# Input loads, square sums and modulation columns at the start of layer 0 of a two-layer hybrid trunk

## The chip, the cores and the metric

The kernel runs on one NeuronCore of one Trainium2 chip. The metric is the device time of one execution in microseconds. The engines are named as in the profile: PE (TensorE) multiplies matrices, PEld is its weight load, DVE is VectorE, ACT is ScalarE, POOL is GpSimd, and SP only issues loads and stores.

## The reference, cut to what matters

Two layers run one after the other on x of 512 positions and 1024 features. Each layer normalises x, scales and shifts it with columns made from a conditioning vector c, multiplies by a wide matrix, runs three attention mixers, and adds the gated result to x:

```
mod = silu(c) @ w_ada + b_ada
shift, scale, gate = split(mod, 3)
u = rms_norm(x, norm_g) * (1 + scale) + shift
z = u @ w_in                      # all queries, keys, values and gates
y = three mixers on z
x = x + gate * (merge(y) @ w_out)
```

rms_norm divides by the root of the mean of the squares of a position's 1024 features. Everything is float32. The change touches the start: the loads of x, the squares, shift and scale of layer 0, and u.

## The kernel before

**Layout.** x is kept transposed: features on the 128 partitions, in eight blocks of 128 (k or j from 0 to 7), positions along the free dimension (512). A float32 product is made of three: u is split into uh (rounded) and ul (the rest), a weight into whi and wlo, and TensorE adds whi with uh, whi with ul and wlo with uh.

**Start.** `start` (lines 1419 to 1483) makes silu(c) and spreads it over a tile csr. Its inner function `norm` (line 1440) is called once for the first 256 positions and once for the second 256 (HALVES). It issues four loads of x (two blocks each, 256 KB, into the tiles vc and va), squares each piece on ScalarE into a tile t, adds the squares up, and lets TensorE sum them over the partitions by a multiplication with a matrix of -1. For the first half VectorE adds all pieces and TensorE does one multiplication; for the second half VectorE or GpSimd adds the two blocks of a piece, and TensorE does four. `rstd_of` (line 761) then makes the inverse root with Ln and Exp on ScalarE. `times_rstd` (765) multiplies x by it on VectorE. `make_u` (768) writes uh and a copy e, each as x * amul + mods, on ScalarE or VectorE, and ul = e - uh.

**Modulation of layer 0.** `ada_load(j)` (718) loads two pieces of 512 KB of w_ada for block j into tiles Y, of which there are five. `ada_first(j)` (723) forms two sums of 1024 products on VectorE, one for shift and one for scale, adds the bias columns into mods, and makes amul = (1 + scale) * norm_g.

**First phase.** `first_phase` (906) runs over the eight blocks. Per block it multiplies seven 128-column tiles of w_in (FIRST) with u: 21 multiplications into seven PSUM banks. In layer 0 blocks 0 and 1 are done in halves of 256 positions (`two0`), the others at the full 512. Before block k + 1 come its modulation, times_rstd and make_u. The weights of a block are two pieces (256 and 192 KB) that go through four wstage tiles and are split by a cast (whi) and a subtraction (wlo). After the first phase come the value projections (`v_phase`), then the mixers, the other projections and the output.

**What sets the order.** The program is first written into a `Recorder` (244) as a list of instructions. `add` (274) derives which instruction must wait for which from the elements of each tile that a view covers; `View.region` (191) gives a view's range of partitions and one range of elements, from the lowest to the highest. `forward` (379) then simulates the engines with a price per instruction (`price`, 307). Where an instruction names two engines, it goes to the one that would end it first. `latest` (500) gives due times, and after five rounds (`order`, 526) the best order is written out (`emit`, 539): each engine's queue runs in that fixed order. SP's queue is ordered in the same way. All emitted instructions carry the line 549, so the profile is read by tiles.

```
        whole = self.tile.at
        p0, f0 = divmod(self.at.__array_interface__["data"][0] - whole.__array_interface__["data"][0], whole.shape[1])
        free = list(zip(self.at.strides[1:], self.at.shape[1:]))
        lo = f0 + sum(min(0, s * (n - 1)) for s, n in free)
        hi = f0 + sum(max(0, s * (n - 1)) for s, n in free) + 1
        return p0, p0 + self.at.shape[0], lo, hi
```

A load of the second half of blocks 0 and 1 writes elements 256 to 511 and 768 to 1023 of its tile; region() calls that 256 to 1023. Elements 512 to 767 are the first half of block 1.

Of the kernel before, what the change touches and what calls it, by code (L numbers as in the profile page):

```python
# [25 lines left out]
F32 = mybir.dt.float32  # L26
F32R = mybir.dt.float32r
BF16 = mybir.dt.bfloat16
AF = mybir.ActivationFunctionType
OP = mybir.AluOpType  # L30

D = 1024
S = 512
P = 128
# [119 lines left out]
class View:  # L154
# [30 lines left out]
    def real(self):  # L185
# [2 lines left out]
            ap = ap.rearrange(arg, a=more[0]) if more else getattr(ap, name)(arg)  # L188
        return ap

    def region(self):

        whole = self.tile.at
# [5 lines that stand above are left out]
# [45 lines left out]
class Recorder:  # L244
# [29 lines left out]
    def add(self, ways):  # L274
        x = Instr()
        x.i = len(self.list)
        op, args, kw = next(iter(ways.values()))
        if op == "pairs":
            named = [(("out", "in", "in")[n], v) for q in args for n, v in enumerate(q)]
        else:  # L280
            named = [("out" if "out" not in kw and n == 0 else n, v) for n, v in enumerate(args)] + list(kw.items())
        x.writes = [v for n, v in named if isinstance(v, View) and n in ("out", "accum_out")]
        x.reads = [v for n, v in named if isinstance(v, View) and n not in ("out", "accum_out")]
        x.preds, x.succs = {}, []
        for views, w in ((x.reads, False), (x.writes, True)):
            for v in views:
                t, r = v.tile, v.region()
                if op == "matmul" and w and kw["start"]:
                    r = (r[0], r[1], 0, S)
                keep = []  # L290
                for (j, r2, w2) in t.seen:
                    over = r[0] < r2[1] and r2[0] < r[1] and r[2] < r2[3] and r2[2] < r[3]
                    if over and j is not x and (w or w2):
                        x.preds[j.i] = j
                    if not (w and over and r[0] <= r2[0] and r2[1] <= r[1] and r[2] <= r2[2] and r2[3] <= r[3] and j is not x):
                        keep.append((j, r2, w2))
                t.seen = keep + [(x, r, w)]
        x.tiles = list({id(v.tile): v.tile for v in x.reads + x.writes if not v.tile.pool.fixed}.values())
        for j in x.preds.values():
            j.succs.append(x)  # L300
        x.alts = {}
        for e, (op, args, kw) in ways.items():
            x.alts[e] = self.price(x, e, op, args, kw)
        x.prio = x.i
        self.list.append(x)
# [266 lines left out]
def trunk(ctx, tc, xT, vecs, w_ss, w_gt, w_first, w_t, w_v, w_br, w_o, rope, consts, out):  # L572
# [6 lines left out]
    rec = Recorder(tc, nc, ps, sb)  # L579
    PE, ACT, DVE, POOL, SP = (rec.engine(e) for e in ("PE", "ACT", "DVE", "POOL", "SP"))  # L580

    def fixed(name, shape, dt=F32):
        return rec.fixed(const.tile(shape, dt, name=name))
# [7 lines left out]
    def ybank():  # L591
        return rec.tile("ps_s", [P, S])
# [4 lines left out]
    def mm(o, lhsT, rhs, start, stop=True):  # L597
        PE.matmul(o, lhsT, rhs, start=start, stop=stop, skip_group_check=True)
# [5 lines left out]
    f = lambda ap: ap.bitcast(F32)  # L604
# [14 lines left out]
    def both(out, a, b, op_):  # L619
        how = ("tensor_tensor", (), dict(out=out, in0=a, in1=b, op=op_))  # L620
        rec.add({"DVE": how} if in_psum(a, b) else {"POOL": how, "DVE": how})
# [12 lines left out]
    csb, o = small[:, 0:8], 8  # L634
    g_sb = [small[:, o + 8 * l:o + 8 * l + 8] for l in range(L)]
    fg_sb, o = small[:, o + 8 * L:o + 8 * L + 8], o + 8 * L + 8
    b_ada, o = [small[:, o + 24 * l:o + 24 * l + 24] for l in range(L)], o + 24 * L
    sink, o = small[:, o:o + 8 * L], o + 8 * L
    ident = small[:, o:o + P]
    nones = fixed("nones", [P, P], F32R)  # L640
# [56 lines left out]
    st = {}  # L697


    mods = [fixed(f"mods{l}", [P, 24], F32) for l in range(L)]  # L700
    amul = [fixed(f"amul{l}", [P, 8], F32) for l in range(L)]
# [21 lines left out]
    def ada_first(j):  # L723
        o = rec.tile("dot", [P, 4], F32)
        for i in range(2):
            w, m = st["wada", j][i], 8 * i + j
            DVE.scalar_tensor_tensor(w, w, 1.0, csr, op0=OP.mult, op1=OP.mult, accum_out=o[:, i:i + 1])
            DVE.tensor_tensor(out=mods[0][:, m:m + 1], in0=o[:, i:i + 1], in1=b_ada[0][:, m:m + 1], op=OP.add)
        DVE.scalar_tensor_tensor(amul[0][:, j:j + 1], mods[0][:, 8 + j:9 + j], 1.0, g_sb[0][:, j:j + 1], op0=OP.add, op1=OP.mult)

    def ada_g(l, j, q):
        def fn(w):
# [35 lines left out]
    def make_u(l, k, xk, cs_=FULL):  # L768
        t = t512("e", 2)[:, cs_]
        sc, sh = amul[l][:, k:k + 1], mods[l][:, k:k + 1]  # L770
        if cs_.start == 0:
            st["uh"][k] = t512(f"uh{k}", 1, F32R)
            st["ul"][k] = t512(f"ul{k}", 1, F32R)
        for o in (st["uh"][k][:, cs_], t):
            rec.add({"ACT": ("activation", (o, xk[:, cs_], AF.Identity), dict(scale=sc, bias=sh)),
                     "DVE": ("tensor_scalar", (o, xk[:, cs_], sc, sh), dict(op0=OP.mult, op1=OP.add))})
        both(st["ul"][k][:, cs_], t, f(st["uh"][k][:, cs_]), OP.subtract)
# [641 lines left out]
    def start():  # L1419
        st["uh"], st["ul"] = [None] * KT, [None] * KT  # L1420
        st["warm"] = ybank()
        for _ in range(WARM):
            mm(st["warm"][:, :P], f(nones), f(nones), True)
        e = fixed("e", [P, 8], F32)
        ACT.activation(e, csb, AF.Exp, scale=-1.0)
        DVE.tensor_scalar(e, e, 1.0e38, 1.0, op0=OP.min, op1=OP.add)
        DVE.reciprocal(e, e)
        DVE.tensor_tensor(out=cs, in0=csb, in1=e, op=OP.mult)
        for h in range(2):
            d, p = t512("t", 10), zbank()  # L1430
            DVE.tensor_tensor(out=d.rearrange("p (a b) -> p a b", a=4), in0=ident.unsqueeze(1).to_broadcast([P, 4, P]),
                                         in1=cs[:, 4 * h:4 * h + 4].unsqueeze(2).to_broadcast([P, 4, P]), op=OP.mult)
            mm(p, f(nones), d, True)
            ACT.activation(csr[:, S * h:S * h + S], p, AF.Copy, scale=-1.0)
        POOL.tensor_scalar(sk8, sink, 8.0, None, op0=OP.mult)
        xx = [rec.tile(t, [P, 4, S], F32) for t in ("vc", "va")]
        x = st["x"] = [xx[k // 4][:, k % 4] for k in range(KT)]
        nb = st["nbank"] = st["rstd"] = sbank()

        def norm(cs_):  # L1440
            for k in range(0, KT, 2):
                SP.dma_start(xx[k // 4][:, k % 4:k % 4 + 2, cs_], xT[:, k:k + 2, cs_])
            prev = None
            for k in range(0, KT, 2):
                t = t512("t", 10)
                a, b = t[:, :S // 2], t[:, S // 2:]
                ACT.activation(t.rearrange("p (a b) -> p a b", a=2), xx[k // 4][:, k % 4:k % 4 + 2, cs_], AF.Square)
                if cs_.start == 0:
                    if k:
                        DVE.tensor_tensor(out=t, in0=t, in1=prev, op=OP.add)  # L1450
                    if k == 6:
                        DVE.tensor_tensor(out=a, in0=a, in1=b, op=OP.add)
                        mm(nb[:, cs_], f(nones), a, True)
                else:
                    both(a, a, b, OP.add)
                    mm(nb[:, cs_], f(nones), a, False, k == 6)
                prev = t
            rstd_of(nb[:, cs_])

        def busy(n, v):  # L1460
            for _ in range(n):
                mm(st["warm"][:, :P], f(nones), v[:, :P], True)

        norm(HALVES[0])
        ada_load(0)
        ch.load(1)
        busy(3, ch.raw[0][0])
        busy(4, ch.raw[1][0])
        ada_first(0)
        for k in (0, 1):  # L1470
            times_rstd(x[k], HALVES[0])
            busy(2, x[k])
        make_u(0, 0, x[0], HALVES[0])
        norm(HALVES[1])
        ada_load(1)
        for k in (0, 1):
            times_rstd(x[k], HALVES[1])
        ada_first(1)
        make_u(0, 1, x[1], HALVES[0])
        make_u(0, 0, x[0], HALVES[1])  # L1480
        make_u(0, 1, x[1], HALVES[1])
        ch.load(3)
        ada_load(2)
# [113 lines left out]
```

## Time and profile before

| what | us |
|---|---|
| median of three runs | 1230.9 (1229.34 to 1233.75) |
| the profiled execution | 1230.21 |
| its span, first to last instruction | 1228.4 |
| PE busy | 1197.8 (98%) |
| DVE busy | 978.2 (80%) |
| ACT busy | 553.4 (45%) |
| POOL busy | 254.3 (21%) |

Times in the profile count from the start of the span. A row of the timeline gives start, length, engine, line, operation, output and inputs, and in brackets how long the engine idled before it and what ended that. A row of the groups gives count, busy time, mean length in ns, and the idle time before them. A busy PE is one with a matmul in its pipeline, and matmuls overlap, so their lengths add up to more than the time that they take.

### The profile page before, as it was taken

How to read it: one execution, taken by the hardware profiler on the slowest of the kernel's cores; microseconds unless marked ns; L12 is line 12 of the kernel's file. 1: busy time of each engine (PE TensorE's matmuls, PEld its weight loads, DVE VectorE, ACT ScalarE, POOL GpSimd, SP SyncE). 2: the span in 40 equal slices, each digit the busy share in tenths (PEclk: the TensorE clock that was granted, in tenths of full speed). 3: DMA queues.
4: the chain of work that ended last, by engine and by line, in shares of the span. 5: the costliest groups of instructions: out<-in, count | busy, mean ns of one | idle time of the engine just before them, and what ended most of it. 6: DMA issues, size and time to landing. Idle time of an engine off the chain costs nothing.

```text
span 1228.4 us, 17793 instructions
## 1 busy us (share of the span) xinstructions
PE 1197.8 (98%) x5984; PEld 971.8 (79%) x5984; DVE 978.2 (80%) x2142; ACT 553.4 (45%) x1152; POOL 254.3 (21%) x283
## 2 busy tenths in 40 slices
PE   5999999999999999999999999999999999999997
PEld 4889877777877887778898987777777778877886
DVE  7976999999888977777475689989997888667654
ACT  4442767555355532542143157665434554234222
POOL 0110344522111111001200015553220110100120
PEclk7999999999999999999999999999999999999999
DMA  9544222233333555343534432224342224322343
GB/s 341 172 120 136 78 78 86 86 113 113 112 102 96 143 150 144 95 120 123 183 117 104 120 106 77 79 77 114 101 129 78 85 87 113 98 66 78 94 122 102
DMA packets 81915, 139.40 MB, mean 113 GB/s; under 512 B 10016, under 2 KB 22560, under 8 KB 81824
## 3 DMA queue, kind: packets, MB, share of 16 engines
q1 hardware_dynamic: 80672, 136.17, 37.7%
q10 hardware_dynamic: 1152, 2.10, 0.5%
q8 instruction: 47, 0.77, 0.3%
q14 instruction: 44, 0.36, 0.1%
HBM read 125.39 MB, written 4.19 MB: 105 GB/s over the span
## 4 chain that ended last, share of the span: by engine, by line
PE 90%; DVE 4%; DMA 2%; ACT 2%; SPq 1%; issue 0%; DVEq 0%
PE ps_z L549 67%; PE ps_s L549 22%; DVE t L549 2%; ACT t L549 1%; PE ps_s L547 1%; DMA vc<-in_xT 1%; SPq L549 1%; DMA m<-zs 1%; DMA Y<-in_w_ss 1%; DVE Q L549 0%; DVE m L549 0%; DVE wlo L549 0%; DVE e L549 0%; DVE zc L549 0%; DVE score L549 0%
## 5 line engine op out<-in xcount | busy, mean ns | idle before, releaser
L549 PE MATMUL ps_z<-uh,whi 128*128 128x512 f32 (+1 forms) x908 | 360.5, 398 | 8.6 <-ACT uh L549 7.6
L549 PE MATMUL ps_z<-uh,wlo 128*128 128x512 f32 (+1 forms) x908 | 356.1, 393 | 0.0
L549 PE MATMUL ps_z<-ul,whi 128*128 128x512 f32 (+1 forms) x908 | 355.8, 392 | 0.0
L549 POOL TENSOR_TENSOR wlo<-wstage,whi 128x512 fp32r<-128x512 f32 (+2 forms) x134 | 176.8, 1320 | 691.0 <-DVE whi L549 333.7
L549 PEld LDWEIGHTS ps_z<-uh,whi 128*128 128x128 f32 x908 | 170.5, 188 | 48.9 <-ACT uh L549 8.1
L549 PEld LDWEIGHTS ps_z<-uh,wlo 128*128 128x128 f32 x908 | 170.8, 188 | 39.1 <-issue 1.0
L549 PEld LDWEIGHTS ps_z<-ul,whi 128*128 128x128 f32 x908 | 170.9, 188 | 36.0 <-issue 1.1
L549 DVE TENSOR_TENSOR wlo<-wstage,whi 128x512 fp32r<-128x512 f32 (+2 forms) x238 | 156.8, 662 | 11.8 <-ACT whi L549 2.6
L549 ACT CAST whi<-wstage 128x512 fp32r<-128x512 f32 (+2 forms) x145 | 86.0, 596 | 171.6 <-PE ps_z L549 113.1
L549 DVE CAST whi<-wstage 128x512 fp32r<-128x512 f32 (+2 forms) x181 | 74.3, 411 | 111.2 <-PE ps_z L549 93.9
L549 PE MATMUL ps_z<-Y,whi 128*128 128x512 f32 x384 | 121.7, 396 | 0.0
L549 ACT ACTIVATE e<-ps_z 128x512 f32<-128x512 f32 x68 | 40.3, 594 | 129.2 <-PE ps_z L549 128.8
L549 PEld LDWEIGHTS ps_z<-Y,whi 128*128 128x128 f32 x384 | 71.7, 188 | 17.0
L549 ACT ACTIVATE e<-e 128x512 f32<-128x512 f32 x96 | 60.5, 632 | 49.4 <-DVE e L549 48.3
L549 PE MATMUL ps_z<-Y,wlo 128*128 128x512 f32 x192 | 75.8, 395 | 0.0
L549 ACT ACTIVATE t<-t 128x512 f32<-128x512 f32 x120 | 71.1, 628 | 8.2 <-POOL t L549 3.1
L549 ACT ACTIVATE t<-t,nm 128x256 f32<-128x256 f32 (+3 forms) x128 | 65.1, 510 | 17.5 <-DVE nm L549 17.2
L549 PE MATMUL ps_s<-small,t 128*128 128x128 f32 x432 | 59.0, 274 | 6.4 <-DVE t L549 3.9
L549 PEld LDWEIGHTS ps_s<-small,t 128*128 128x128 f32 x432 | 50.0, 141 | 17.9 <-DVE t L549 6.0
L549 POOL CAST whi<-wstage 128x512 fp32r<-128x512 f32 (+1 forms) x46 | 28.9, 629 | 161.6 <-PE ps_z L549 83.5
L549 DVE SCALAR_TENSOR_TENSOR wstage<-wstage,csr 128x512 f32<-128x512 f32 x64 | 50.5, 790 | 6.0 <-DMA wstage<-in_w_ss 4.0
L549 DVE MAX8 m<-score 128x8 f32<-128x256 f32 (+2 forms) x96 | 53.4, 556 | 1.6
(212 smaller groups left out, 2058.0 us busy)
## 6 DMA issues: line engine op xcount, KB each, us to landing
wstage<-in_w_t SPq DMA_DIRECT2D x212, 256.0 KB, 2.7
wstage<-in_w_v SPq DMA_DIRECT2D x48, 182.0 KB, 2.4
Y<-in_w_ss SPq DMA_DIRECT2D x16, 512.0 KB, 7.5
m<-zs SPq DMA_DIRECT2D x128, 64.0 KB, 2.0
wstage<-in_w_gt SPq DMA_DIRECT2D x32, 256.0 KB, 2.6
wstage<-in_w_ss SPq DMA_DIRECT2D x32, 256.0 KB, 2.7
wstage<-in_w_o SPq DMA_DIRECT2D x32, 256.0 KB, 2.7
wstage<-in_w_first SPq DMA_DIRECT2D x16, 256.0 KB, 3.2
```

What stands on the lines that cost most here:

```text
L547: self.real[engine].matmul(*[real(a) for a in q], start=False, stop=True, skip_group_check=True)
L549: getattr(self.real[engine], y.op)(*[real(a) for a in y.args], **{k: real(v) for k, v in y.kw.items()})
```

## The change

- `View.regions` is new: a view of two to eight rows with gaps between them is given as one range per row, and `add` compares these ranges.
- `norm`: the adds on VectorE and GpSimd are gone. TensorE takes each block's squares by themselves: eight multiplications per half.
- `ada_first`: the shift column is sum + bias, and amul is sum * norm_g + gb, where gb = (1 + bias) * norm_g is made once at the start. Each is one instruction on ScalarE or VectorE (`linear`).
- `make_u`: in layer 0 uh and e are made on ScalarE only.
- The second half's loads stand in the program where they stood; with the finer ranges the planner queues them right behind the first weights.

```diff
+    def regions(self):
+
+        if len(self.at.shape) == 3 and 1 < self.at.shape[1] <= 8 and self.at.strides[1] > self.at.shape[2] * self.at.strides[2] > 0:
+            return [self[:, n].region() for n in range(self.at.shape[1])]
+        return [self.region()]
...
-            for v in views:
-                t, r = v.tile, v.region()
+            for v, r in [(v, r) for v in views for r in v.regions()]:
+                t = v.tile
...
-            w, m = st["wada", j][i], 8 * i + j
+            w = st["wada", j][i]
             DVE.scalar_tensor_tensor(w, w, 1.0, csr, op0=OP.mult, op1=OP.mult, accum_out=o[:, i:i + 1])
-            DVE.tensor_tensor(out=mods[0][:, m:m + 1], in0=o[:, i:i + 1], in1=b_ada[0][:, m:m + 1], op=OP.add)
-        DVE.scalar_tensor_tensor(amul[0][:, j:j + 1], mods[0][:, 8 + j:9 + j], 1.0, g_sb[0][:, j:j + 1], op0=OP.add, op1=OP.mult)
+        g = g_sb[0][:, j:j + 1]
+        linear(mods[0][:, j:j + 1], o[:, 0:1], None, b_ada[0][:, j:j + 1])
+        linear(amul[0][:, j:j + 1], o[:, 1:2], g, st["gb"][:, j:j + 1])
+
+    def linear(o, x, scale, bias):
+
+        if scale is None:
+            rec.add({"ACT": ("activation", (o, x, AF.Identity), dict(bias=bias)), "DVE": ("tensor_tensor", (), dict(out=o, in0=x, in1=bias, op=OP.add))})
+        else:
+            rec.add({"ACT": ("activation", (o, x, AF.Identity), dict(bias=bias, scale=scale)), "DVE": ("tensor_scalar", (o, x, scale, bias), dict(op0=OP.mult, op1=OP.add))})
...
         for o in (st["uh"][k][:, cs_], t):
+            if l == 0:
+                ACT.activation(o, xk[:, cs_], AF.Identity, scale=sc, bias=sh)
+                continue
...
+        gb = st["gb"] = fixed("gb", [P, 8], F32)
+        DVE.scalar_tensor_tensor(gb, b_ada[0][:, 8:16], 1.0, g_sb[0], op0=OP.add, op1=OP.mult)
...
-            prev = None
             for k in range(0, KT, 2):
                 t = t512("t", 10)
-                a, b = t[:, :S // 2], t[:, S // 2:]
                 ACT.activation(t.rearrange("p (a b) -> p a b", a=2), xx[k // 4][:, k % 4:k % 4 + 2, cs_], AF.Square)
-                if cs_.start == 0:
-                    if k:
-                        DVE.tensor_tensor(out=t, in0=t, in1=prev, op=OP.add)
-                    if k == 6:
-                        DVE.tensor_tensor(out=a, in0=a, in1=b, op=OP.add)
-                        mm(nb[:, cs_], f(nones), a, True)
-                else:
-                    both(a, a, b, OP.add)
-                    mm(nb[:, cs_], f(nones), a, False, k == 6)
-                prev = t
+                for i in range(2):
+                    mm(nb[:, cs_], f(nones), t[:, 256 * i:256 * i + 256], cs_.start == 0 and k + i == 0, k + i == 7)
```

## Rows read from the trace of the kernel before

**Rows 1.** The page's 40 slices: busy tenths of PE and of DMA.
```profile
PE   5999999999999999999999999999999999999997
...
DMA  9544222233333555343534432224342224322343
```

**Rows 2.** Table of stretches: length, busy us per engine, granted clock, DMA share, GB/s.
```profile
25.00:30.00 5.00, 4.15 (x13) 3.68 (x14) 3.53 (x10) 0.80 (x2) 0.00 (x0) 0.50 1.06 387
...
33.15:67.00 33.85, 33.85 (x167) 28.59 (x168) 30.54 (x63) 14.91 (x24) 5.97 (x7) 1.00 0.49 151
0.00:33.15 33.15, 20.09 (x94) 17.25 (x94) 23.07 (x58) 13.96 (x26) 1.30 (x8) 0.79 0.97 341
...
80.00:1212.00 1132.00, 1124.42 (x5602) 908.07 (x5601) 906.59 (x1982) 512.51 (x1079) 244.09 (x265) 1.00 0.36 105
```

**Rows 3.** Timeline from 16 to 34 us, the rows around TensorE's long stop.
```profile
16.66 0.38 SPq L549 DMA_DIRECT2D vc<-in_xT  x1
...
17.87 0.16 DVE L549 SCALAR_TENSOR_TENSOR amul<-mods,small 128x1 f32<-128x1 f32 x1
...
24.18 0.63 ACT L549 ACTIVATE t<-vc 128x512 f32<-128x512 f32 x1 [4.05 <-DMA vc<-in_xT]
...
25.21 0.58 ACT L549 ACTIVATE uh<-vc,mods,amul 128x256 fp32r<-128x256 f32 x1
...
25.85 0.80 PE L549 MATMUL ps_z<-uh,whi 128*128 128x256 f32 x2 [7.61 <-ACT uh L549]
...
27.51 3.62 PE L549 MATMUL ps_s<-t,nones 128*128 128x256 f32 x8
...
31.16 0.45 ACT L549 ACTIVATE ps_s<-ps_s,epst 128x256 f32<-128x256 f32 x1 [5.37 <-PE ps_s L549]
...
33.15 0.51 PE L549 MATMUL ps_z<-uh,whi 128*128 128x256 f32 x2
```

**Rows 4.** Table of stretches, from VectorE's first modulation sum to its last ul.
```profile
9.64:33.15 23.51, 14.67 (x74) 13.15 (x74) 18.65 (x48) 8.98 (x18) 0.00 (x0) 0.71 1.05 377
33.15:62.97 29.82, 29.82 (x150) 25.22 (x151) 28.11 (x58) 12.65 (x20) 5.43 (x6) 1.00 0.48 153
sum 53.33, PE 44.48 PEld 38.37 DVE 46.76 ACT 21.63 POOL 5.43; mean PE 22.24 PEld 19.18 DVE 23.38 ACT 10.81 POOL 2.72
```

**Rows 5.** DMA issues of x: count, KB each, median us to landing.
```profile
vc<-in_xT SPq DMA_DIRECT2D x4, 256.0 KB, 5.2
```

**Rows 6.** Timeline, TensorE's first use of the first weights.
```profile
11.47 3.31 PE L549 MATMUL ps_s<-wstage,nones 128*128 128x128 f32 x14 [0.93 <-DMA wstage<-in_w_first]
```

**Rows 7.** Timeline, the first half's one sum of squares.
```profile
9.87 0.67 PE L549 MATMUL ps_s<-t,nones 128*128 128x256 f32 x2 [3.42 <-DVE t L549]
```

**Rows 8.** Groups of VectorE's instructions from 9.64 to 62.97 us.
```profile
L549 DVE TENSOR_TENSOR mods<-dot,small 128x1 f32<-128x1 f32 x16 | 3.5, 218 | 0.4
...
L549 DVE TENSOR_TENSOR t<-t 128x256 f32<-128x256 f32 x5 | 2.1, 426 | 0.9 <-ACT t L549 0.7
L549 DVE TENSOR_SCALAR e<-va,amul,mods 128x512 f32<-128x512 f32 x3 | 1.6, 542 | 0.0
...
L549 DVE SCALAR_TENSOR_TENSOR amul<-mods,small 128x1 f32<-128x1 f32 x8 | 1.3, 159 | 0.3
...
L549 DVE TENSOR_SCALAR e<-vc,amul,mods 128x256 f32<-128x256 f32 (+1 forms) x2 | 0.9, 472 | 0.0
L549 DVE TENSOR_SCALAR uh<-vc,amul,mods 128x256 fp32r<-128x256 f32 x1 | 0.4, 406 | 0.0
```

**Rows 9.** Groups of ScalarE's instructions, 9.64 to 62.97 us; the last row from 0 to 9.64.
```profile
L549 ACT CAST whi<-wstage 128x512 fp32r<-128x512 f32 (+2 forms) x15 | 8.3, 569 | 14.5 <-PE ps_s L549 6.9 <-PE ps_z L549 6.5 <-DMA wstage<-in_w_first 0.7
...
L549 ACT ACTIVATE uh<-va,mods,amul 128x512 fp32r<-128x512 f32 x4 | 3.3, 818 | 3.5 <-DVE amul L549 3.5
...
L549 ACT ACTIVATE e<-va,mods,amul 128x512 f32<-128x512 f32 x1 | 0.8, 799 | 0.0
...
L549 ACT ACTIVATE e<-small 128x8 f32<-128x8 f32 x1 | 0.2, 208 | 0.8 <-DMA small<-in_vecs 0.8
```

**Rows 10.** Who waited for whom: TensorE from 34 us on; us in total, times, longest.
```profile
PE ps_s L549 <- DVE t L549: 3.9, 4, 2.0
```

## The prediction

> **What bounds the kernel now.** I read the 40 slices of the page first. TensorE is full in all slices but the first and the last, and DMA is full only in the first one [rows 1]. So the kernel is bound by TensorE nearly throughout, and a change to the start is worth what it takes out of the start. The table of stretches [rows 2] gives sizes: TensorE idles 13.1 us of the first 33.15 (33.15 less 20.09), nothing from 33.15 to 67.00, and 7.6 us in the 1132 us from 80 to 1212. From 33.15 to about 67.00 it runs the rest of layer 0's first phase without a gap: the second half (256 of the 512 sequence columns) of feature blocks 0 and 1, then blocks 2 to 7 at full width. That is 14 half-width blocks in 33.85 us, 2.4 us each.
>
> Then the start, instruction by instruction [rows 3]. TensorE stops for 7.61 us before 25.85, waiting for uh (scaled input) of block 1, first half. Its modulation columns were ready at 18.03 (17.87 + 0.16). But on ScalarE that uh stands behind the square of the last piece of the second half, which waited 4.05 us for its load. That load was issued at 16.66 and landed at 24.18. The cause is in the planner: region() turns a view of two rows with a gap into one range from its first to its last element, so a load of the second half of blocks 0 and 1 seems to overwrite block 1's first half. The load is ordered behind that half's readers, and uh of block 1 behind the load. From 25.85 TensorE works at half clock (0.50 granted from 25 to 30 [rows 2]): four sums of squares take 3.62 us, 0.9 each, and end at 31.13; its first multiplication of the second half comes at 33.15, 2.0 us later (Ln, Exp, one multiplication by rstd, uh).
>
> VectorE is the second limit. From its first modulation sum at 9.64 to the last ul at 62.97 it is busy 46.76 of 53.33 us, and in the second part 28.11 of 29.82, while ScalarE is busy 21.63 [rows 4]. So an earlier start of TensorE is worth only what VectorE can follow.
>
> **The change part by part.**
>
> *Loads.* The second half's four loads (256 KB each, 1.05 MB [rows 5]) go behind the first weights, past the two sums' weights of block 1, two pieces of first-phase weights and what follows them on SP. Issuing costs nothing new: the same loads on the same queue. The first weights' first piece landed at 11.47, the second (192 KB) some 0.5 us later; the core moved 377 GB/s in this stretch [rows 4, 6]. So the second half lands at 12.0 + 2.8 = 14.8 instead of 24.18, and everything it passes comes 2.8 us later. Who waits for that: VectorE's sums for block 1. It has other work there (splitting the first weights, two multiplications by rstd, a ul), so I charge at most 1 us, and nothing if that cover holds; without it the price is the whole 2.8.
>
> *Squares.* From 11.47 ScalarE has two casts (0.57 each), uh and e (0.58 each), two small columns (0.21 each) and four squares (0.63 each): 5.2 us, so the last square ends about 16.7 [rows 3, 9]. Per half there are now eight sums on TensorE: seven more in the first half, four more in the second. At 0.45 (full clock, half of 0.9) to 0.9 us that is 5 to 10 us of TensorE, but all but the last two run while TensorE would wait for input, where it idles 13.1 us. The two behind the last square cost 0.9 to 1.8: sums done at 17.6 to 18.5. With the 2.0 us from the last sum to the first multiplication, TensorE starts the second half at 19.6 to 20.5; I take 20. In the first half the sum today waits 3.42 us for VectorE's chain of adds [rows 7]. That goes, but it only lets block 0's first half run earlier into the wait for the second, so I count it as nothing.
>
> *Sum on TensorE.* From 20 on it has block 1's first half (2.4, done before 33.15 today) and the 33.85: the phase ends at 56.3 instead of 67.0, 10.7 earlier. Against that stands the clock: after the 7.61 us of idling the 5.3 us to 31.13 ran at half speed (1.2 instead of 2.4 GHz), a loss of up to 2.6. The new gap is about 2 us with sums inside it. I take a loss of 1 between 0 and 2.6: 9.7 earlier.
>
> *Sum on VectorE.* Gone: four adds of squares (4 x 0.43 = 1.7), 16 shift and scale columns (3.5), 8 amul (1.3), and scaled input (1.6 + 0.9 + 0.4 = 2.9) [rows 8]. Together 9.4 of its 46.8 us. One 128x8 product for gb comes, 0.2 us at most, in front of 9.64, where VectorE waits anyway. Were the columns left on VectorE (the planner may choose), only 4.6 would go. Its own wait for rstd of the second half shrinks, its wait for block 1's weights grows by up to 1. So the last ul comes about 9 us earlier, which is what block 7 needs. VectorE and TensorE agree, so I take **9 us**.
>
> *ScalarE.* It gains four full-width and two half-width ACTIVATEs (0.80 and 0.58: 4.4 us) and 16 (sums' own columns plus amul) at 0.21, with 0.45 the other end (an ACTIVATE with a bias column on 256 elements is the nearest longer row [rows 3]): 3.4 to 7.2. So 21.6 becomes 29 to 33 of some 44 us. It is not the bound if its order is right. One row speaks against the move: uh and e cost 0.82 and 0.80 on ScalarE, 0.54 on VectorE [rows 8, 9]. The Trainium skill (ScalarE: Activation LUTs, section Rules for kernel authors) says the same as a rule: additions and multiplications belong on VectorE, not on ScalarE. By that rule the moved scaling would lose some 1.4 us of engine time; the trace agrees on the price, but ScalarE is the engine with room. If the 1.4 us stood on the path, the forecast below would be 1222.9.
>
> *Rest of the kernel.* The planner orders all that follows anew. Its work is the same, and TensorE is full there, so I add nothing; what it may cost is a rival.
>
> The profiled execution took 1230.2 us (span 1228.4), 0.7 below the median of the three runs. 1230.2 less 9 is 1221.2; on the median's scale 1221.9. I forecast **1221.5 us**.
>
> **The rivals.**
>
> *A: ScalarE and VectorE take turns (slower).* Place: blocks 2 to 7. If VectorE's queue has ul right behind the sums on which it now depends by way of ScalarE (columns 0.21, uh 0.82, e 0.80: 1.8 us), it idles that long in each block. Its own work per block is (46.8 - 9.4) / 8 = 4.7, so a block takes 6.5 us instead of 4.8: 6 x 1.7 = 10 us, which eats the whole gain (1231). And TensorE then pauses in each block; a block at half clock takes 9.7 us instead of 6.5, and if two of the six fall to it, that is 6.4 more: about 1237. It decides when the idle per block is over about 1.5 us. For it: the order is fixed beforehand and each queue is in order. Against: today VectorE waits only 1.7 us of 29.8 [rows 4] with the same dependences, and ScalarE already makes uh of blocks 4 to 7 from VectorE's columns [rows 9]. Chance 0.08.
>
> *B: the gain is given back later.* A new order of the 1132 us from 80 to 1212 needs only 4 to 8 more us of TensorE idling on top of today's 7.6, of which 3.9 are waits for VectorE's t [rows 2, 10]. Time: 1225.5 to 1229.5. For it: from 240 on small reorderings do show as waits. Against: it is 99% full there under the same rules. Chance 0.14.
>
> *C: half the gain.* The loads do not go as early as said (or block 1's weights, now 2.8 us later, hold VectorE), and only the freed uh of block 1 counts. The last square then still ends at 24.81 (24.18 + 0.63); with two sums behind it (1.8) and the 2.0 the second half starts at 28.6 instead of 33.15, block 1's first half being done in the idle time before: 4.5 us, 1225.7, with the unknowns 1225 to 1227. Chance 0.10.
>
> *Forecast*, 1217 to 1225: 0.68. The low end is the 10.7 with no loss of clock (1219.5) and 2 to 3 us more if the planner also fills later gaps.
>
> **How the numbers follow.** A difference within 0.3% (3.7 us) is about what a measurement of this kernel can tell from none: 1227.2 to 1234.6. Faster: the forecast, C and a third of B, 0.68 + 0.10 + 0.05 = 0.83. Same: the rest of B and the mild end of A, 0.09 + 0.02 = 0.11. Slower: the rest of A, 0.06. The range reaches from 1216.5 to 1228.5: it takes in both ends of the unknown costs, C and most of B.
>
> **What would show it.** In the changed profile: the four second-half loads landed by about 15; uh of block 1's first half not behind a square; TensorE without a gap from about 20, and the first phase ending near 58; VectorE without mods, amul and TENSOR_SCALAR before that, its last ul near 54; ScalarE near 30 us busy there. I am wrong if TensorE pauses between blocks (A), if the phase ends at 58 but the span does not follow (B), or if the loads land after 18 (C).

## The result and the profile after

| | before | after |
|---|---|---|
| median, us | 1229.78 (1228.37 to 1233.75) | 1220.88 (1218.73 to 1221.94) |
| ratio, 95% interval | | 0.9922 [0.9905, 0.9939] |
| profiled execution, us (its span) | 1230.21 (1228.4) | 1218.73 (1216.9) |
| end of the first phase | 67.31 | 57.37 |
| span behind that point | 1161.1 | 1159.5 |

8.9 us faster by the medians, 0.8%, more than twice the 0.3% that can be told from none. As end of the first phase I take the transposes behind its last block, since they are easy to find in every kernel (`ps_s<-small,zs`). They come 9.94 us earlier; the rest is 1.6 shorter in these two executions, and a later section shows that a difference of this size means nothing.

First the page's 40 slices, of after (answers [rows 1]).

```profile
PE   9999999999999999999999999999999999999997
...
PEclk9999999999999999999999999999999999999999
DMA  9644322434434445245533532224342224322343
```

The first slice of PE went from 5 to 9, the clock row has no dip. The timeline of after, from 13 us to the end of the phase, answers [rows 3].

```profile
15.03 1.14 ACT L555 ACTIVATE t<-va 128x512 f32<-128x512 f32 x2
...
15.54 2.75 PE L555 MATMUL ps_s<-t,nones 128*128 128x256 f32 x12
...
16.32 1.23 DVE L555 SCALAR_TENSOR_TENSOR Y<-Y,csr 128x1024 f32<-128x1024 f32 x1 [1.26 <-DMA Y<-in_w_ss]
...
17.94 0.47 PE L555 MATMUL ps_z<-uh,wlo 128*128 128x256 f32 x1
...
18.36 0.62 ACT L555 CAST whi<-wstage 128x512 fp32r<-128x512 f32 x1 [2.20 <-DMA wstage<-in_w_first]
...
18.89 0.44 ACT L555 ACTIVATE ps_s<-ps_s,epst 128x256 f32<-128x256 f32 x1
...
19.62 0.27 DVE L555 TENSOR_SCALAR amul<-dot,small,gb 128x1 f32<-128x1 f32 x1
...
19.96 0.58 ACT L555 ACTIVATE uh<-vc,mods,amul 128x256 fp32r<-128x256 f32 x1
...
20.27 1.94 DVE L555 TENSOR_TENSOR vc<-vc,ps_s 128x256 f32<-128x256 f32 x4
...
20.60 0.39 PE L555 MATMUL ps_z<-uh,whi 128*128 128x256 f32 x1
...
20.94 0.59 ACT L555 ACTIVATE uh<-vc,mods,amul 128x256 fp32r<-128x256 f32 x1
...
52.84 0.69 DVE L555 TENSOR_TENSOR ul<-e,uh 128x512 fp32r<-128x512 f32 x1
...
57.37 0.60 PE L555 MATMUL ps_s<-small,zs 128*128 128x128 f32 x4
```

The last square of the second half ends at 16.17 (15.03 + 1.14), not at 24.81. The sums follow one another until 18.29. Ln starts 0.6 later, because it stands behind the cast at 18.36, which had waited 2.20 us for weights. At 20.60 TensorE begins block 1, and the phase ends 36.77 us later. The stop of 7.61 us is gone.

What begins at 20.60 is still the first half: its uh is the one at 19.96, right behind block 1's column amul (19.62), while the multiplications by the second half's rstd start only at 20.27. The second half's first uh is the one at 20.94; it is done at 21.53, 3.2 us after the last sum. TensorE does not stand still for that: behind the sums it runs block 0's first half (from 17.94; the row before 20.60 ends at 20.56), then block 1's.

The table of stretches of after, from VectorE's first modulation sum to its last ul (answers [rows 4]):

```profile
9.53:53.53 44.00, 43.53 (x240) 37.40 (x239) 38.79 (x71) 27.35 (x56) 7.88 (x9) 1.00 0.90 312
```

The stretch is 9.33 us shorter than before. VectorE is occupied 7.97 us less in it (46.76 less 38.79) and idles 1.36 less. TensorE misses 0.47 us. Groups of ScalarE in the same stretch of after (answers [rows 8, 9]):

```profile
L555 ACT ACTIVATE amul<-dot,gb,small 128x1 f32<-128x1 f32 x7 | 2.7, 382 | 2.5 <-DVE Y L555 2.5
...
L555 ACT ACTIVATE mods<-dot,small 128x1 f32<-128x1 f32 x7 | 2.0, 292 | 1.3 <-DVE Y L555 1.3
```

The planner put seven of the eight column pairs on ScalarE. A column takes 292 or 382 ns there, not the 208 of [rows 9]. The Trainium skill (ScalarE: Activation LUTs, section Rules for kernel authors) gives about 0.3 us per ACTIVATE plus a share per element; the trace agrees with 0.292 for the plain one.

### The profile page after: what moved, and what is told of

It reads as the page before. It is cut to its first block, busy times and chain, and to the rows that moved or that the text cites. A ratio compares the mean times of both kernels' runs of the same rounds, so it can differ in the third digit from the quotient of the medians.

```text
span 1216.9 us, 17822 instructions
## 1 busy us (share of the span) xinstructions
PE 1200.1 (99%) x6006; PEld 973.3 (80%) x6006; DVE 963.6 (79%) x2105; ACT 559.2 (46%) x1171; POOL 257.5 (21%) x286
## 4 chain that ended last, share of the span: by engine, by line
PE 90%; DVE 4%; SPq 2%; ACT 1%; DMA 1%; issue 1%; DVEq 0%
PE ps_z L555 68%; PE ps_s L555 21%; SPq L555 2%; DVE t L555 1%; PE ps_s L553 1%; ACT t L555 1%; DMA m<-zs 1%; DMA wstage<-in_w_first 1%; DVE Q L555 1%; DVE m L555 0%; DVE wlo L555 0%; DVE e L555 0%; DVE zc L555 0%; DVE zs L555 0%; DVE whi L555 0%
## 5 line engine op out<-in xcount | busy, mean ns | idle before, releaser
L555 POOL TENSOR_TENSOR wlo<-wstage,whi 128x512 fp32r<-128x512 f32 (+1 forms) x133 | 174.8, 1315 | 661.0 <-DVE whi L555 296.4
L555 POOL CAST whi<-wstage 128x512 fp32r<-128x512 f32 (+2 forms) x47 | 30.0, 638 | 172.1 <-PE ps_z L555 82.3
```

Source lines behind the costliest of these rows:

```text
L555: getattr(self.real[engine], y.op)(*[real(a) for a in y.args], **{k: real(v) for k, v in y.kw.items()})
```

## The experiments

All are measured against the kernel before. "Ln" is the start of the second half's Ln, "ul" the start of the last ul, "end" that of the transposes, "rest" the span behind it; these are of one profiled execution each.

| kernel | median, us | ratio, 95% interval | Ln | ul | end | rest |
|---|---|---|---|---|---|---|
| before | 1229.78 | | 31.16 | 62.27 | 67.31 | 1161.1 |
| after | 1220.88 | 0.9922 [0.9905, 0.9939] | 18.89 | 52.84 | 57.37 | 1159.5 |
| e1_ranges_alone | 1227.09 | 0.9972 [0.9963, 0.9981] | 20.49 | 58.78 | 63.67 | 1161.6 |
| e2_all_but_ranges | 1227.45 | 0.9979 [0.9969, 0.9989] | 29.28 | 56.50 | 66.12 | 1158.6 |
| e3_old_adds | 1224.32 | 0.9953 [0.9939, 0.9966] | 20.70 | 56.11 | 60.68 | 1162.3 |
| e4_old_columns_u | 1224.38 | 0.9954 [0.9941, 0.9966] | 18.16 | 56.36 | 60.85 | 1161.7 |
| e5_adds_and_dummies | 1220.65 | 0.9917 [0.9904, 0.9931] | 19.02 | 52.31 | 58.16 | 1158.4 |
| e6_loads_first | 1222.52 | 0.9936 [0.9923, 0.9950] | 18.71 | 53.28 | 58.17 | 1161.6 |
| e7_free_u | 1222.95 | 0.9939 [0.9927, 0.9952] | 18.75 | 57.16 | 61.73 | 1160.3 |
| e8_late_loads | 1220.14 | 0.9915 [0.9901, 0.9928] | 21.86 | 52.40 | 59.91 | 1159.2 |
| e9_ranges_and_dummies | 1229.58 | 1.0001 [0.9993, 1.0010] | 20.74 | 58.29 | 63.25 | 1164.8 |
| e10_old_columns | 1222.35 | 0.9943 [0.9931, 0.9955] | 18.66 | 55.09 | 59.52 | 1160.5 |
| e11_changed_again | 1220.09 | 0.9926 [0.9914, 0.9938] | 18.95 | 52.91 | 57.43 | 1161.9 |
| e12_loads_first_own_bank | 1220.36 | 0.9919 [0.9902, 0.9936] | 18.62 | 53.23 | 58.12 | 1162.2 |

### The two halves of the change, each alone

The theory is that the early loads carry the gain and the rest makes it possible for VectorE to follow; the rival is that the two parts add up. The first kernel is the kernel before with the finer ranges only:

```diff
-            for v in views:
-                t, r = v.tile, v.region()
+            for v, r in [(v, r) for v in views for r in v.regions()]:
+                t = v.tile
```

> The kernel before with the finer ranges alone: the second half's loads go early, sums, columns and scaled input stay as they were. My theory (TensorE can start the second half near 21, but VectorE keeps its 46.8 us of work and only loses the waits for the second half): last ul near 59 instead of 62.97, first phase ends near 63 instead of 67.3, gain 3 to 5 us, ratio to before 0.996 to 0.9975. Rival 'the early loads are the whole gain': first phase ends near 58, gain 8 to 10 us, ratio 0.992 to 0.9935. Rival 'VectorE's load is the whole gain': gain under 2 us, ratio over 0.9985.

The second is the changed kernel without them:

```diff
-            for v, r in [(v, r) for v in views for r in v.regions()]:
+            for v, r in [(v, v.region()) for v in views]:
```

> The changed kernel with the one range per view of before: the second half's loads go late again (last landing near 24), sums, columns and scaled input as changed. My theory: the last square ends near 24.8, sums and rstd bring the second half's start to near 27.7, VectorE is not the limit; first phase ends at 61.5 (block 1's first half done before) to 64, gain 3 to 5.5 us, ratio 0.9955 to 0.9975. Rival 'the early loads are the whole gain': gain under 2 us. Rival 'VectorE's load is the whole gain': gain 8 to 10 us, ratio 0.992 to 0.9935.

The early loads alone bring the end from 67.31 to 63.67 (3.6), all the rest alone to 66.12 (1.2). Together they bring 9.9, so 5.1 us of it exist only together. By the medians it is 2.9, 2.6 and 8.9, so 3.4 only together. The first expectation held. The second missed: I had said 61.5 to 64 for the end, and 0.9955 to 0.9975 for the ratio. Stretches of e1_ranges_alone show where it stops:

```profile
10.00:15.00 5.00, 3.58 (x16) 3.18 (x17) 4.84 (x10) 3.42 (x7) 2.23 (x2) 0.64 1.08 372
15.00:20.00 5.00, 5.00 (x26) 4.84 (x26) 4.35 (x11) 1.25 (x3) 0.00 (x0) 0.68 1.06 386
...
40.00:45.00 5.00, 3.87 (x17) 2.85 (x16) 4.97 (x10) 1.23 (x2) 2.23 (x3) 1.00 0.81 291
45.00:50.00 5.00, 4.69 (x21) 3.32 (x20) 4.93 (x10) 1.85 (x3) 2.06 (x2) 1.00 0.93 330
50.00:55.00 5.00, 3.86 (x17) 2.88 (x16) 4.90 (x12) 1.85 (x3) 0.00 (x0) 1.00 0.20 65
```

Ln came 10.7 us earlier than before (20.49 instead of 31.16), the end only 3.6. From 40 to 55 TensorE has pauses, while VectorE (third engine column) is occupied 4.90 to 4.97 of every 5 us and ScalarE 1.2 to 1.9. VectorE is the limit. In the timeline of e2_all_but_ranges the other limit is seen:

```profile
23.40 0.63 ACT L555 ACTIVATE t<-vc 128x512 f32<-128x512 f32 x1 [3.51 <-DMA vc<-in_xT]
...
24.08 5.16 PE L555 MATMUL ps_s<-t,nones 128*128 128x256 f32 x16 [6.86 <-ACT t L555]
...
29.28 0.45 ACT L555 ACTIVATE ps_s<-ps_s,epst 128x256 f32<-128x256 f32 x1 [2.87 <-PE ps_s L555]
```

The late load is that of the first piece, and TensorE takes the sums in the written order. So all eight sums of the half wait for it, and they then run for 5.16 us: from 20 to 25 the granted clock was 0.52, from 25 to 30 it was 0.80. I had priced two sums behind the last square, not eight: in this kernel the sums on TensorE stand on the path when the loads are late.

### Sums on TensorE or on VectorE, and the clock

The changed kernel with the old adds on VectorE and GpSimd:

```diff
-                for i in range(2):
-                    mm(nb[:, cs_], f(nones), t[:, 256 * i:256 * i + 256], cs_.start == 0 and k + i == 0, k + i == 7)
+                if cs_.start == 0:
...
+                else:
+                    both(a, a, b, OP.add)
+                    mm(nb[:, cs_], f(nones), a, False, k == 6)
```

> The changed kernel with the adds of squares back on VectorE and GpSimd (one sum on TensorE for the first half, four for the second). My theory: the chain of squares is 0.5 to 1 us longer, and TensorE idles between 6.5 and 9.8 and again before the second half, so that its clock falls and 1 to 2.6 us of full-speed work are lost; first phase ends 1 to 3 us after that of the changed kernel (57.4), ratio to before 0.993 to 0.9955. Rival 'the sums on TensorE cost what they add (11 more multiplications, 5 us)': first phase ends earlier than 57.4.

The end came at 60.68, 3.3 later than after. Either the adds cost VectorE its 1.7 us and a wait, or TensorE loses its clock when it has no sums to do. To tell these apart, e5_adds_and_dummies keeps the old adds and lets TensorE multiply the raw x by the same matrix, into a bank that nobody reads; this is added work, not part of the computation. The kernel before already does this with the first weights.

```diff
                 for i in range(2):
+                    mm(st["warm"][:, :256], f(nones), xx[k // 4][:, k % 4 + i, cs_], True)
```

> The adds of squares back on VectorE and GpSimd as in the run with the old adds (whose first phase ended at 60.68), and TensorE gets as many multiplications as the changed kernel has sums, on the loaded x, with a result that nobody reads. Clock theory: the granted clock stays at 1.00 from 5 us on, most of the 3.3 us to the changed kernel (57.37) comes back, first phase ends at 58 to 59. Rival 'the chain of adds costs it': first phase ends at 60 to 61.5 although the clock is up.

Stretches of e3_old_adds, then of e5_adds_and_dummies (the granted clock is third from the right):

```profile
5.00:10.00 5.00, 2.48 (x5) 0.94 (x4) 2.65 (x5) 2.63 (x5) 0.00 (x0) 0.90 0.95 308
10.00:15.00 5.00, 3.83 (x16) 3.15 (x15) 4.00 (x9) 3.87 (x9) 1.33 (x1) 0.50 1.08 367
...
20.00:25.00 5.00, 3.14 (x16) 2.74 (x16) 3.61 (x8) 4.23 (x10) 1.21 (x1) 0.76 1.06 386
25.00:30.00 5.00, 5.00 (x40) 5.00 (x40) 3.41 (x9) 2.71 (x6) 0.00 (x0) 0.89 1.04 329
```

```profile
5.00:10.00 5.00, 5.00 (x18) 3.53 (x17) 3.18 (x5) 2.83 (x5) 0.00 (x0) 1.00 0.98 321
10.00:15.00 5.00, 5.00 (x35) 4.48 (x34) 4.32 (x10) 4.00 (x10) 0.51 (x1) 1.00 1.07 369
...
20.00:25.00 5.00, 5.00 (x45) 5.00 (x43) 4.96 (x11) 3.84 (x9) 1.17 (x2) 1.00 1.06 386
25.00:30.00 5.00, 5.00 (x40) 4.78 (x38) 3.91 (x7) 4.37 (x9) 0.00 (x0) 1.00 1.05 385
```

With TensorE occupied, the granted clock stays at 1.00 (2.4 GHz), and the end goes from 60.68 to 58.16. These 2.5 us of the 3.3 have two parts. Timeline of e3_old_adds, then TensorE's first row of block 1 in e5_adds_and_dummies:

```profile
20.70 0.45 ACT L555 ACTIVATE ps_s<-ps_s,epst 128x256 f32<-128x256 f32 x1 [1.33 <-PE ps_s L555]
...
21.46 0.38 ACT L555 ACTIVATE amul<-dot,gb,small 128x1 f32<-128x1 f32 x1
...
22.52 0.72 PE L555 MATMUL ps_z<-uh,whi 128*128 128x256 f32 x2 [1.86 <-ACT uh L555]
```

```profile
21.32 0.40 PE L555 MATMUL ps_z<-uh,whi 128*128 128x256 f32 x2
```

From block 1 to the end TensorE takes 38.16 us in e3 and 36.84 in e5: 1.3 us in the multiplications themselves, which is the clock (0.76 and 0.89 from 20 to 30 us, against 1.00). The other 1.2 us are a later start. In e3 block 1's uh waits for its amul, which stands behind Ln on ScalarE, and Ln waits 1.33 us for the last sum; in e5 the planner made that amul on VectorE. How much of the 1.2 us is the slower TensorE and how much the new order is not shown. The remaining 0.8 to the changed kernel is for the most part a later start too (block 1 at 21.32 instead of 20.60), and e5's time (0.9917) is that of the changed kernel. So the sums matter here mainly as work that keeps TensorE occupied.

Is it the clock, too, that limits the early loads alone? e1 ran from 10 to 20 at 0.64 and 0.68. So I added the same multiplications to it (the edit of e1 and the line of e5):

> The kernel before with the finer ranges, and with 16 multiplications on TensorE on the loaded x whose result nobody reads. The run with the finer ranges alone ended its first phase at 63.67 with the clock down between 10 and 20 us. Theory (VectorE with its old work is what holds that run): the clock stays at 1.00, but the first phase ends within 1 us of 63.67, ratio to before 0.996 to 0.998. Rival 'the clock holds it': first phase ends at 61 to 62, as in the pair with the old adds, where the same multiplications gave 2.5 us.

The clock stayed at 1.00 through the phase, but the end came at 63.25 instead of 63.67. VectorE's limit holds there, as that theory said. The total missed what I had expected (0.996 to 0.998): 1.0001 of before, though the phase ends 4.1 us earlier in the profiled execution. The whole front gain is given back behind it. Stretches of e9_ranges_and_dummies, then of the kernel before:

```profile
66.00:240.00 174.00, 171.88 (x930) 143.73 (x929) 147.03 (x298) 95.34 (x179) 55.17 (x77) 1.00 0.34 97
240.00:400.00 160.00, 154.12 (x748) 120.53 (x748) 140.66 (x345) 79.72 (x198) 37.65 (x31) 0.99 0.37 105
```

```profile
66.00:240.00 174.00, 172.43 (x936) 144.32 (x935) 148.47 (x292) 95.90 (x180) 56.25 (x79) 1.00 0.33 96
240.00:400.00 160.00, 156.69 (x767) 122.82 (x766) 143.06 (x361) 82.75 (x201) 38.22 (x33) 1.00 0.37 108
```

TensorE idles 8.0 us in these 334 us (2.12 and 5.88) against 4.9 before (1.57 and 3.31), in one execution each. Who waited for whom, TensorE of e9_ranges_and_dummies from 66 us on (us in total, times, longest), answers [rows 10]:

```profile
PE ps_s L555 <- DVE t L555: 4.9, 5, 2.3
PE ps_s L555 <- DVE wlo L555: 2.5, 2, 2.1
PE ps_z L555 <- ACT e L555: 2.3, 2, 1.7
```

This is rival B, in another kernel than the one I predicted: the program behind the phase is the same, only the order is new, and the engine where the planner may choose one.

### Columns and scaled input: ScalarE or VectorE

Three kernels go back on the two moves: both of them, u alone (free to go to either engine), the columns alone.

```diff
-        linear(mods[0][:, j:j + 1], o[:, 0:1], None, b_ada[0][:, j:j + 1])
-        linear(amul[0][:, j:j + 1], o[:, 1:2], g, st["gb"][:, j:j + 1])
+            DVE.tensor_tensor(out=mods[0][:, m:m + 1], in0=o[:, i:i + 1], in1=b_ada[0][:, m:m + 1], op=OP.add)
+        DVE.scalar_tensor_tensor(amul[0][:, j:j + 1], mods[0][:, 8 + j:9 + j], 1.0, g_sb[0][:, j:j + 1], op0=OP.add, op1=OP.mult)
...
-            if l == 0:
-                ACT.activation(o, xk[:, cs_], AF.Identity, scale=sc, bias=sh)
-                continue
```

> The changed kernel with the modulation columns on VectorE as before and the scaled input free for either engine as before. My theory: VectorE has 7.7 us more to do and is the limit again; its last ul comes 3 to 6 us later than in the changed kernel, the first phase ends at 60 to 63, ratio to before 0.995 to 0.9975. Rival 'the early loads are the whole gain': first phase ends within 1 us of 57.4, ratio 0.992 to 0.9935.

> The changed kernel with the scaled input of layer 0 free for either engine, columns as changed. Theory (VectorE's work counts): VectorE takes some of it, up to 2.9 us more work, first phase ends at 57.4 to 60. Together with the run of old columns and free u (60.85) it splits the 3.5 us: I expect 1 to 1.5 us for the scaled input and the rest for the columns. Rival 'the planner does as well without the rule': within 0.5 us of 57.4.

> The changed kernel with the columns on VectorE as before and the scaled input on ScalarE as changed. VectorE has 4.8 us more to do than in the changed kernel, but waits for ScalarE only before each ul, not for the columns. Theory: first phase ends at 58.5 to 60.5, later than the changed kernel's 57.4 and earlier than with free u and new columns (61.5), where VectorE and ScalarE wait for each other in turns; ratio to before 0.993 to 0.9955. Rival 'the columns' place alone makes the difference': as the run with old columns and free u, 60.85 or later.

Against the end of after, 57.37: both back cost 3.5 us (60.85), the columns alone 2.1 (59.52), u alone 4.4 (61.73). e4 and e10 came as expected, e7 did not: by the end of the phase, to give the planner its choice back for u is worse than to undo both moves. The totals do not show that: e7 has 0.9939, e4 0.9954, and their intervals overlap. Of the three only e4 has an interval apart from that of after. In the timeline of e7_free_u:

```profile
37.53 0.62 ACT L555 CAST whi<-wstage 128x512 fp32r<-128x512 f32 x1 [4.09 <-DMA wstage<-in_w_first]
...
38.26 1.07 ACT L555 CAST whi<-wstage 128x384 fp32r<-128x384 f32 x2
...
39.24 0.38 ACT L555 ACTIVATE amul<-dot,gb,small 128x1 f32<-128x1 f32 x1
39.65 0.81 ACT L555 ACTIVATE uh<-va,mods,amul 128x512 fp32r<-128x512 f32 x1
39.65 0.55 DVE L555 TENSOR_SCALAR e<-va,amul,mods 128x512 f32<-128x512 f32 x1 [1.72 <-ACT amul L555]
...
40.52 0.72 PE L555 MATMUL ps_z<-uh,whi 128*128 128x512 f32 x2 [1.58 <-ACT uh L555]
```

VectorE makes the modulation sum, ScalarE the column from it, and then VectorE waits 1.72 us for this column, since it stands behind casts on ScalarE, the first of which had waited 4.09 us for its weights. TensorE waits another 1.58 us for uh. From 20 to 62 us VectorE waited 4.2 us for ScalarE's amul, in four places. This is rival A's mechanism, but not the whole price: VectorE also took uh and e of 6.5 us of length back, against 3.7 in e4. In the changed kernel uh and e are on the same engine as the column that they need, and VectorE comes back only for ul; TensorE has no such waits there. So at the end of the phase the two moves belong together: with u on ScalarE the columns there are worth 2.1 us (e10 against after), with u left free they cost 0.9 (e7 against e4).

On the price alone VectorE is better: 0.54 us per instruction against 0.82 [rows 8, 9], and the rule that I weighed (Trainium skill, ScalarE: Activation LUTs, Rules for kernel authors) says so. By time it is not: e4, which goes back towards it, ends the phase 3.5 us later, and its ratio is 0.9954 against 0.9922. Another page of the Trainium skill (Perfetto Trace Analysis, section Optimizing Scalar/DVE Operations) makes the exception: with a saturated VectorE, moving work to ScalarE may make sense. The trace agrees, with 4.90 us of 5 on VectorE from 40 to 55 in e4.

### Where in the queue the loads go

The change puts the second half's loads behind the first weights. Two kernels put them elsewhere in the program: ahead of everything, or behind the weights of block 1, both those of its sums and those of its first phase. For this the loads move out of `norm` into a function of their own, `load_x`.

```diff
+        load_x(HALVES[0])
+        load_x(HALVES[1])
         norm(HALVES[0])
```

> The changed kernel with the second half's loads directly behind the first half's, ahead of the modulation and first-phase weights of block 0. Theory: the second half lands near 10.7, all other weights of block 0 2.8 us later; block 0 starts near 16 with both halves and TensorE goes on without a wait: first phase ends at 55 to 57, ratio to the changed kernel 0.998 to 1.0. Rival 'VectorE is already the limit': its last ul stays within 0.7 us of 52.84 and the first phase ends at 57 to 58.5. Rival 'the gap at the front lets the clock fall': granted clock under 0.8 between 10 and 20, first phase ends after 58.

```diff
+        ada_load(1)
+        ch.load(3)
+        load_x(HALVES[1])
         norm(HALVES[1])
-        ada_load(1)
```

> The changed kernel with the second half's loads behind the modulation and first-phase weights of block 1 (1.5 MB, 4.0 us at 377 GB/s). Theory: the last square ends near 20.5 instead of 16.2, the second half starts near 24.5 instead of 20.6; block 1's first half can run before it, 2.4 us; first phase ends 1.5 to 4 us after 57.4, ratio to before 0.994 to 0.997. Rival 'the place in the queue hardly matters once the ranges are right': first phase ends within 1 us of 57.4.

Ahead of everything brings nothing: Ln at 18.71 (after: 18.89), end at 58.17 and not at the 55 to 57 that I expected. Later costs 2.5 us at the end of the phase (59.91), as expected, with Ln 3.0 later. Yet its time, 0.9915 and not 0.994 to 0.997, is not behind that of the changed kernel. The 2.5 us at the front do not reach the total.

In e6 the two halves' sums share one PSUM bank, and I suspected that the second half waits for the first one's Ln and Exp there. So the last experiment gives the second half a bank of its own, with the loads still first:

```diff
+                    own = nb if cs_.start == 0 else zbank()
...
+                    mm(own[:, cs_], f(nones), t[:, 256 * i:256 * i + 256], k + i == 0, k + i == 7)
...
```

> Edit: the changed kernel with the second half's loads ahead of everything in the first weights' place, as in e6_loads_first, and the sums of the second half in a PSUM bank of their own, so that they no longer wait for Ln, Exp and the multiplication by rstd of the first half. If VectorE's queue is the limit of the first phase: the Ln of the second half comes earlier than e6's 18.71 (16 to 18), but the last ul stays within 1 us of 52.8 and the phase ends at 57 to 58.5; the time is that of the changed kernel within 2 us. If the shared bank is what kept e6 from gaining: the last ul comes 1.5 us or more before 52.8 and the phase ends at 54.5 to 56, 1.5 to 3 us faster than the changed kernel.

Ln came at 18.62, 0.1 earlier than e6's and not in the 16 to 18 that I expected. So the bank was not what came last. The timeline of e12_loads_first_own_bank shows what was:

```profile
11.27 1.15 ACT L555 ACTIVATE t<-va 128x512 f32<-128x512 f32 x2
...
12.51 3.19 PE L555 MATMUL ps_z<-t,nones 128*128 128x256 f32 x14
...
12.95 1.23 DVE L555 SCALAR_TENSOR_TENSOR Y<-Y,csr 128x1024 f32<-128x1024 f32 x1 [8.12 <-DMA Y<-in_w_ss]
...
15.53 1.72 PE L555 MATMUL ps_s<-wstage,nones 128*128 128x128 f32 x14
...
17.09 1.06 PE L555 MATMUL ps_s<-vc,nones 128*128 128x128 f32 x8
...
17.98 0.60 PE L555 MATMUL ps_z<-t,nones 128*128 128x256 f32 x2
...
21.56 0.50 PE L555 MATMUL ps_z<-uh,whi 128*128 128x256 f32 x2 [0.48 <-ACT uh L555]
```

The squares are done at 12.42, and seven of the eight sums by 15.70. The last one comes only at 17.98: the planner put the unread multiplications (`wstage`, `vc`) ahead of it in TensorE's queue. And the loads that went first pushed VectorE's input back: its first modulation sum starts at 12.95 instead of 9.53. DMA is full from 5 to 30 us (shares of 1.00 to 1.06), so whatever goes earlier there pushes something else back. VectorE makes up for most of this (24.73 us of 25 occupied from 20 to 45, against 23.00 in after), and the last ul comes 0.4 later. Yet that ul is not what holds the end: TensorE comes to block 1 at 21.56, 1.0 later than in after, and has no pause from 25 to 55 us (30.00 us of 30 busy). That the end stays at 57 to 58.5 fits the expectation for VectorE's queue, but TensorE's later start is what the trace shows.

### The changed kernel once more

> The changed kernel again, to see how far its executions and its profile differ from the first ones: first phase ends within 0.5 us of 57.37, median 1219.5 to 1221.5, ratio 0.991 to 0.9935. If the median comes out at or under 1220.2, the run with the late loads (1220.1, first phase 2.5 us later) is slower at the front and not faster in all; if it is above 1220.5, what that run loses at the front it gets back later.

The same kernel gave 0.9926, with a median of 1220.09. That is under the 1220.2 drawn beforehand, so e8 is slower at the front and not faster in all. The end is at 57.43 here, within 0.06; but its rest is 1161.9 against 1159.5. So 2.4 us of rest can lie between two executions of one kernel, and the 1.6 by which the first was shorter than before is no gain. Over all kernels the rest runs from 1158.4 to 1164.8.

No kernel is measurably faster than the changed one: the best of the others, e8 and e5, have 0.9915 and 0.9917 with intervals that hold 0.9922.

## Why the prediction was right

The forecast of 1221.5 us stands against 1220.88, for mostly the reasons given. One term was wrong (the clock), and at one place the number came by another path than the one I had worked out. Step by step:

- **Loads, squares, sums.** Right. The last squares start at 15.03 without a wait for their loads (landing said: 14.8). The last square ends at 16.17 (said: 16.7), the sums at 18.29 (17.6 to 18.5). The wait of VectorE for block 1's weights, charged with at most 1 us, is 1.26.
- **"TensorE starts the second half at 19.6 to 20.5; I take 20".** TensorE comes to block 1 and all behind it at 20.60, close to the 20 of the sum. The path is not the one worked out, and that the two agree is luck. The chain from the last sum to the second half's first uh took 3.2 us and not 2.0 (18.29 to 21.53), since Ln stood behind the cast that waited for weights, a second cast ran between Ln and Exp (19.25), and the multiplications by rstd came behind VectorE's work for block 1. The cast's weights are among what the loads passed in SP's queue; I had looked for the price of that at VectorE and not at ScalarE's queue. It cost nothing, because TensorE was not waiting. I had counted block 0's first half as done by then; in truth it stood behind the sums and ran from 17.94 to 20.56, through the wait that I had priced. What starts at 20.60 is block 1's first half, and what it waited for last was uh at 19.96, behind block 1's amul.
- **Sum on TensorE.** The predicted 2.4 + 33.85 = 36.25 us of work came out as 36.77, from 20.60. Of the 0.5 more, 0.3 is the mark of the end: 67.31 before by the transposes, where I had taken 67.0.
- **"I take a loss of 1 between 0 and 2.6" for the clock.** The term that was wrong: the loss is 0. The granted clock is 1.00 in every 5 us from 0 to 65. I had called the further sums a cost that is hidden. They are what holds the clock, and without them the phase ends 2.5 us later, of which 1.3 is surely the clock (e3 against e5). Before, it ran at 0.50 after the stop. The loss I charged and the delay I did not charge (0.6 at the start, 0.2 in the work) nearly cancel: 9.94 measured against 9.7.
- **Sum on VectorE, 9.4.** Right in the instructions, too large as time. The groups of [rows 8] are lengths, and VectorE's instructions overlap: over the stretch all groups added up to 52.8 us before, while VectorE was occupied 46.76, and to 43.3 after, while it was occupied 38.79. The lengths fell by 9.5, the occupied time by 8.0. The last ul came 9.4 earlier all the same, as VectorE also idled 1.4 less.
- **"VectorE and TensorE agree."** Right. TensorE has no pause worth naming from 20.60 to the end. And from the end of the last ul to the end of the phase there are 3.84 us (57.37 less 53.53), while in the kernels in which TensorE paused for u (e4, e7, e10) it is 3.75 to 3.88. By this sign both limits meet at 57.4; e5 and e8 have 5.2 and 6.8 there, where TensorE ends it alone.
- **ScalarE 29 to 33 us.** 27.35, for the same reason as at VectorE: the lengths of its groups rose by 8.1 (22.9 to 31.0), within the 7.8 to 11.6 of the working, but its occupied time by 5.7 only. The columns lay between the ends given, 0.21 and 0.45. It is not the bound, as said.
- **Rival A** did not occur here, but its mechanism is real: e7 shows it with pauses of up to 1.6 us on TensorE and 1.7 on VectorE, in a kernel that ends the phase 4.4 us later, in part for other reasons. I had priced it at 10 us, for all six blocks; it struck in four waits. The place was another, too: not ul behind uh and e, but e and uh on VectorE behind amul on ScalarE.
- **Rival B** did not occur here either, but did in e9, where 4.1 us were given back. A chance of 0.14 was not too much.
- **Rival C** did not occur: the loads went where the text on the change says.

What stays open: why the order that the planner finds for the rest is 3 us worse in e9 than in others. It is a matter of one fixed order, and I tried no kernel in which the front is changed and the order of the rest held.

## What to carry to other kernels

Before you move an input forward, ask which two engines it will feed: here the loads alone brought the end of the phase 3.6 us forward, the rest of the change alone 1.2, both together 9.9. If a chain goes from VectorE to ScalarE and back, move the consumers with the column, or leave it alone: that is what the end of the phase says here, the totals are too close to. And where a plan is drawn up anew, read the end of the changed phase and the rest apart, since the rest can take back all that the front gave.

## What the hardware showed that I had not expected

- Multiplications whose result nobody reads brought the end of the phase 2.5 us forward, 1.3 of it in the speed of TensorE's own work: with them the granted clock stayed at 1.00 from 5 to 30 us, without them it was 0.50 to 0.92 (e5 and e3). The Trainium skill (TensorE: Matmul & The Clock Gate, section on the HAM clock gate) states the two levels and that idling lowers the clock; the trace agrees with 0.50, the lower level, in e3 from 10 to 15, after 5 us in which TensorE was occupied for 2.48.
- The same held clock brought 0.4 us where VectorE was the limit (63.67 and 63.25 in e1 and e9).
- ScalarE needs 0.29 to 0.38 us for a column of one element per partition, VectorE 0.16 to 0.27 in after.
